# Attention scores laid out keys by queries: the maximum found beforehand, sums over keys divided out in the merge, no transposes of the exponentials

## The chip, the core and the metric

The kernel runs on one core of a Trainium2 chip. The metric is the device time in microseconds of one execution, as the median of several. The core has five engines that work side by side, each through its own list of instructions in order: TensorE (PE in the profile; its weight loads are listed apart as PEld), VectorE (DVE), ScalarE (ACT), GpSimd (POOL) and SyncE (SP), which here only starts DMA transfers. Matrix products go into PSUM, eight banks of 512 float32 columns on 128 partitions; everything else lives in SBUF.

## The reference

One encoder layer is run on two sequences with shared weights: a sample of 1024 tokens and a prompt of 256, each with 16 learned meta tokens in front. What the change touches is the attention:

```python
def attention_block(qb, k, v):
    scale = HEAD_DIM ** -0.5
    s = jnp.einsum('bqhgd,bshd->bhgqs', qb, k).astype(jnp.float32) * scale
    p = jax.nn.softmax(s, axis=-1).astype(v.dtype)
    return jnp.einsum('bhgqs,bshd->bqhgd', p, v)
...
    a = bidirectional_gqa(q, k, v) @ w_attn_o
    fo = fourier_mix(f) @ w_four_o
    merged = g_attn * a + g_four * fo
    x = x + merged @ w_out
```

There are 8 query heads of 64 features; four of them share each of 2 key heads. Queries and keys are normalised per head and rotated before. The gates `g_attn` and `g_four` are sigmoids of further columns of the input projection. A SwiGLU block with two normalisations follows; the change leaves it alone.

## The kernel before

All values are float32. A float32 factor is split into a high and a low part of the type float32r, and a product of two is three products (high by high, high by low, low by high): the helper `three`, lines 218 to 220. The program goes through stages: normalisation and Fourier input; the Fourier branch; keys, values and queries; attention; merge (gated sum of both branches) and output projection; SwiGLU. The attention stage is written out by hand: on TensorE, ScalarE and VectorE the order of the program is the order of the engine, while POOL and SP are ordered by a scheduler, as is everything after attention. SBUF is handed out as equal slots (`Slots`).

Attention works on units: a tile of 128 queries (eight of the sample, two of the prompt, which come first) and one key head. For each of the unit's four query heads, six matmuls give the scores, queries on the partitions and the 1040 keys (272 for the prompt) along the columns (line 898). High and low parts of 64 features stand on top of each other, so that each of the two products contracts over all 128 rows. VectorE finds the maximum over the keys (L903), ScalarE takes the exponential with the maximum as bias and sums it (L910), VectorE divides by the sum (L914, L915). Since the product with the values contracts over the keys, the exponentials are then turned round: for each tile of 128 keys (and one of the 16 meta keys) four transposes, one for each head (L832), a copy of the high part (L834), the low part (L835), and two products with the values (L852, L853). This second half of a unit runs between the score steps of the next one.

Between these steps the program puts matmuls of the gate logits (`gate_gen`, lines 218 to 220 under the names g, hT and wg), work that needs nothing from attention. The table `FILL` says how much after each step: 640 stands for three products of 512 columns. What is not for TensorE of that work goes to ScalarE (L443, L450) and POOL (L444). Gate products that are left over run after attention, while the first inputs of the merge are loaded (`load_af`) and split.

## Time and profile before

| what | value |
|---|---|
| median of 3 runs | 1740.58 us (1740.29 to 1740.63) |
| span of the profiled execution | 1737.8 us |
| instructions | 25952 |
| TensorE busy | 1697.8 us, 98% of the span |
| VectorE, ScalarE, POOL busy | 1140.9, 720.6, 239.6 us |
| first and last score product (L898) | 316.1 us, 637.4 us |
| first product of the merge | 670.9 us |

For the profiled execution the page gives the span, from the first to the last instruction; the median of the runs lies 2.8 us above it. In the rows of the profile, `L898 PE MATMUL S<-kT,qT` is the instruction of line 898 on TensorE that writes tile S from kT and qT; `128*128 128x264` means 128 rows contracted, 128 columns of weights, and a moving tile of 264 columns. In the timeline the first number is the start in us, the second the duration; `x6` joins six instructions that follow each other. In groups by line, the two numbers after the bar are the busy time in us and the mean duration in ns.

### The profile page before, as it was taken

How to read it: one execution, taken by the hardware profiler on the slowest of the kernel's cores; microseconds unless marked ns; L12 is line 12 of the kernel's file. 1: busy time of each engine (PE TensorE's matmuls, PEld its weight loads, DVE VectorE, ACT ScalarE, POOL GpSimd, SP SyncE). 2: the span in 40 equal slices, each digit the busy share in tenths (PEclk: the TensorE clock that was granted, in tenths of full speed). 3: DMA queues.
4: the chain of work that ended last, by engine and by line, in shares of the span. 5: the costliest groups of instructions: out<-in, count | busy, mean ns of one | idle time of the engine just before them, and what ended most of it. 6: DMA issues, size and time to landing. Idle time of an engine off the chain costs nothing.

```text
span 1737.8 us, 25952 instructions
## 1 busy us (share of the span) xinstructions
PE 1697.8 (98%) x9917; PEld 1511.1 (87%) x9917; DVE 1140.9 (66%) x2084; ACT 720.6 (41%) x1391; POOL 239.6 (14%) x239
## 2 busy tenths in 40 slices
PE   7999999999999999999999999999999999999997
...
GB/s 190 63 149 162 116 116 55 122 74 67 70 61 59 61 79 352 250 119 170 145 182 64 85 82 95 90 96 89 94 98 84 71 126 255 198 182 101 159 97 153
DMA packets 100292, 212.06 MB, mean 122 GB/s; under 512 B 10373, under 2 KB 46877, under 8 KB 100168
## 3 DMA queue, kind: packets, MB, share of 16 engines
...
## 4 chain that ended last, share of the span: by engine, by line
PE 67%; DVE 7%; DMA 3%; issue 3%; ACT 1%; POOL 1%; SPq 0%; POOLq 0%; DVEq 0%; ACTq 0%
PE i L218 9%; PE i L220 9%; PE i L219 9%; PE o L220 5%; PE o L219 5%; PE o L218 5%; PE S L898 4%; PE pt L832 4%; PE g L218 2%; PE pv L852 2%; PE g L219 2%; PE g L220 2%; PE pv L853 2%; PE wo L220 2%; PE wo L219 2%
## 5 line engine op out<-in xcount | busy, mean ns | idle before, releaser
L1227 ACT CAST w<-wi 128x512 fp32r<-128x512 f32 x168 | 104.0, 621 | 274.0 <-PE i L220 218.0
L218 PE MATMUL i<-A,w 128*128 128x384 f32 x616 | 208.4, 338 | 3.0 <-ACT w L1227 2.6
L220 PE MATMUL i<-A,w 128*128 128x384 f32 x616 | 208.1, 338 | 2.3 <-POOL w L1229 2.3
L219 PE MATMUL i<-A,w 128*128 128x384 f32 x616 | 207.9, 338 | 0.0
L218 PE MATMUL i<-Ah,w 128*128 128x256 f32 x616 | 173.0, 281 | 1.6 <-DVE sc L1283 1.5
L220 PE MATMUL i<-Ah,w 128*128 128x256 f32 x616 | 173.2, 281 | 0.0
L219 PE MATMUL i<-Al,w 128*128 128x256 f32 x616 | 172.9, 281 | 0.0
L834 ACT CAST pT<-pt 128x512 fp32r<-128x512 f32 x156 | 90.7, 582 | 97.1 <-PE pt L832 94.3
L835 DVE TENSOR_TENSOR pT<-pt,pT 128x512 fp32r<-128x512 f32 x156 | 106.9, 686 | 34.2 <-ACT pT L834 33.0
L1229 DVE TENSOR_TENSOR w<-wi,w 128x512 fp32r<-128x512 f32 x154 | 105.3, 685 | 28.7 <-ACT w L1227 28.3
L903 DVE TENSOR_REDUCE sm<-S 128x1 f32<-128x1040 f32 (+1 forms) x80 | 86.5, 1082 | 50.7 <-PE S L898 47.4
L218 PEld LDWEIGHTS i<-A,w 128*128 128x128 f32 x616 | 116.5, 189 | 3.6 <-ACT w L1227 2.9
L220 PEld LDWEIGHTS i<-A,w 128*128 128x128 f32 x616 | 116.4, 189 | 3.2 <-POOL w L1229 3.2
L218 PEld LDWEIGHTS i<-Ah,w 128*128 128x128 f32 x616 | 116.0, 188 | 2.2 <-DVE sc L1283 1.7
L219 PEld LDWEIGHTS i<-A,w 128*128 128x128 f32 x616 | 116.3, 189 | 0.0
L219 PEld LDWEIGHTS i<-Al,w 128*128 128x128 f32 x616 | 116.2, 189 | 0.0
L220 PEld LDWEIGHTS i<-Ah,w 128*128 128x128 f32 x616 | 116.0, 188 | 0.0
L227 POOL TENSOR_SCALAR fin0r<-fin0ss 128x1 f32<-128x1 f32 x1 | 0.8, 788 | 755.8 <-ACT X L235 755.8
L910 ACT ACTIVATE p<-S,sm 128x1040 f32<-128x1040 f32 (+1 forms) x80 | 80.2, 1003 | 33.6 <-DVE sm L903 27.0
L832 PE MATMUL pt<-ident,p 128*128 128x128 f32 (+1 forms) x624 | 93.4, 272 | 0.0
L220 PE MATMUL o<-wfo,act 128*128 128x512 f32 (+1 forms) x212 | 82.1, 388 | 2.1 <-DVE act L1361 2.1
L219 PE MATMUL o<-wfo,act 128*128 128x512 f32 (+1 forms) x212 | 81.9, 386 | 0.0
...
## 6 DMA issues: line engine op xcount, KB each, us to landing
...
```

The source lines that it names most:

```text
L218: mm(out, sh, mh, start=first and i == 0, stop=False)
L219: mm(out, sh, ml, start=False, stop=False)
L220: mm(out, slo, mh, start=False, stop=last and i == n - 1)
L832: nc.tensor.transpose(pt[:rows, h * P : (h + 1) * P], me.ps4[h][:, col : col + rows], self.ident[:])
L834: nc.scalar.copy(pT[:rows, :512], pt[:rows, :])
L835: nc.vector.tensor_tensor(pT[:rows, 512:1024], pt[:rows, :], f32(pT[:rows, :512]), op=ALU.subtract)
L852: nc.tensor.matmul(me.pv[:], vst, pT[:rows, :512], start=j == 0, stop=False)
L898: nc.tensor.matmul(S[:, base + lo : base + hi], hq, self.kT[seq][g][v][:, lo:hi], start=v == 0, stop=v == 1)
L903: nc.vector.tensor_reduce(nb, S[:, base : base + L], axis=AX.X, op=ALU.max, negate=True)
L910: self.last_exp = nc.scalar.activation(p, S[:, base : base + L], AF.Exp, bias=nb, accum_out=total)
L1227: nc.scalar.copy(w[:, :512], src)
L1229: eng.tensor_tensor(w[:, 512:1024], src, f32(w[:, :512]), op=ALU.subtract)
```

## The change

The scores are made the other way round: keys on the partitions, the 512 queries of the unit's four heads along the columns (L948, L949 of the new kernel). So their exponentials are already what the product with the values needs, and the transposes are gone, with the division. Three things have to be got in another way.

- **The shift.** The maximum over keys now runs across partitions. A first, coarser set of scores (high parts alone, 64 rows, queries on the partitions) is made two units ahead: matmuls in pairs, one head on rows 0 to 63 and one on rows 64 to 127 (L845, L846), four 16-column ones for the meta keys (L854), with maxima by VectorE. The negated maximum is transposed into a row (L865), and four DMAs put it below the queries' high parts as row 64; row 64 of the keys' low part is 1. So the second score product contracts 65 rows and adds the shift.
- **The sums over keys.** VectorE adds the exponentials of all key tiles into a PSUM bank (L970, L972); a product with ones sums over the partitions (L914, L915), ScalarE copies (L918), a DMA stores the row.
- **The division.** The stored sums are read back as a small tile, VectorE takes reciprocals, and they are stored again. In `load_af` products with a 0/1 table of 8 rows spread them over the heads' features (L1073, L1074), and VectorE multiplies the attention output by them (L1076), for each of the three chunks of tokens.

The low part of the exponentials moves from VectorE to POOL, the source of the cast from PSUM to SBUF. PSUM in attention becomes two banks S for the shift and the totals, two for the scores, one each for values and sums, two for gates. Queries are loaded twice in part. The fill becomes 700 after each of nine key tiles in place of 640 after each of eight half steps.

```diff
+        self.tot_d = self.dram.tile([80, P], F32, name="tot_d")
+        self.rc_d = self.dram.tile([80, P], F32, name="rc_d")
...
-    FILL = {"s": 640, "p": 400, "end": 640, "drain": 900}
+    FILL = {"s": 700, "p": 400, "end": 700, "drain": 900}
...
+            nc.gpsimd.memset(f32(k4[:rows, :, 1, 1, :]), 0.0)
+            nc.gpsimd.memset(f32(k4[:rows, :, 1, 1, 0:1]), 1.0)
             nc.scalar.copy(k4[:rows, :, 0, 0, :], kr[:rows])
-            nc.vector.tensor_tensor(k4[:rows, :, 0, 1, :], kr[:rows], f32(k4[:rows, :, 0, 0, :]), op=ALU.subtract)
-            nc.scalar.copy(k4[:rows, :, 1, 1, :], kr[:rows])
+            nc.scalar.copy(k4[:rows, :, 0, 1, :], kr[:rows])
...
+            t = tiles[i]
+            q1, q2 = sl.get("qT", F32R), sl.get("qT2", F32R)
+            nc.sync.dma_start(f32(q1[:, :1024]), self.q_d[t][:])
+            nc.sync.dma_start(f32(q2[:HD, :1024]), self.q_d[t][:HD, :])
+            odd = self.q_d[t][:HD, :].rearrange("d (g p x n) -> d g p x n", g=2, p=2, x=2)
+            for g in range(2):
+                nc.sync.dma_start(
+                    f32(q2[HD:P, g * 512 : g * 512 + 256].rearrange("d (p n) -> d p n", p=2)), odd[:, g, :, 1, :]
+                )
+            q[t] = q1, q2
...
+        def shift_work(t, g):
+            q1, q2 = q[t]
+            kt = self.kT["s" if t < 8 else "p"][g][0]
+            cuts = [(0, 512), (512, 1024)] if t < 8 else [(0, LP)]
+            parts = self.small.tile([P, 4, 4], F32, tag="parts", name=f"mx{t}{g}", bufs=3)
+            def pair(p, i):
+                lo, hi = cuts[i]
+                pp = [ps.tile([P, 512], F32, tag="S", name=f"S{t}{g}{p}{i}{x}") for x in range(2)]
+                h = 4 * g + 2 * p
+                c = g * 512 + p * P
+                nc.tensor.matmul(pp[0][:, : hi - lo], q1[:HD, h * P : (h + 1) * P], kt[:HD, lo:hi], start=True, stop=True)
+                nc.tensor.matmul(pp[1][:, : hi - lo], q2[HD:P, c : c + P], kt[HD:P, lo:hi], start=True, stop=True)
+                for x in range(2):
+                    nc.vector.tensor_reduce(parts[:, 2 * p + x, i : i + 1], pp[x][:, : hi - lo], axis=AX.X, op=ALU.max)
+            def meta():
+                pm = ps.tile([P, 512], F32, tag="S", name=f"S{t}{g}m")
                 for h in range(4):
+                    c = (4 * g + h) * P
+                    nc.tensor.matmul(
+                        pm[:, h * N_META : (h + 1) * N_META], q1[:HD, c : c + P], kt[:HD, SEQ_S:LS], start=True, stop=True
+                    )
+                nc.vector.tensor_reduce(
+                    parts[:, :, 2], pm[:, : 4 * N_META].rearrange("p (h n) -> p h n", h=4), axis=AX.X, op=ALU.max
+                )
+            nb = self.small.tile([P, 4], F32, tag="nb", name=f"nb{t}{g}", bufs=3)
+            def row():
+                pt = ps.tile([P, 512], F32, tag="S", name=f"S{t}{g}r")
+                nc.tensor.transpose(pt[:4, :P], nb[:], self.ident[:])
+                mr = self.small.tile([4, P], F32R, tag="mr", name=f"mr{t}{g}", bufs=1)
+                nc.vector.tensor_copy(mr[:], pt[:4, :P])
+                for h in range(4):
+                    c = (4 * g + h) * P
+                    nc.sync.dma_start(f32(q2[HD : HD + 1, c : c + P]), f32(mr[h : h + 1, :]))
+            for i in range(len(cuts)):
+                for p in range(2):
+                    pair(p, i)
+                    yield
+            if t < 8:
+                meta()
+            n = 3 if t < 8 else 1
+            nc.vector.tensor_reduce(nb[:], parts[:, :, :n], axis=AX.X, op=ALU.max, negate=True)
+            yield
+            row()
+            yield
...
+        def total(unit):
+            t, g, st = unit
+            b = ps.tile([P, 512], F32, tag="S", name=f"S{t}{g}t")
+            a = st["a"]
+            nc.tensor.matmul(b[:2, :], self.ones[:], a[:, :512], start=True, stop=False)
+            nc.tensor.matmul(b[:2, :], self.ones[:], a[:, 512:1024], start=False, stop=True)
+            sl.put(a)
+            s = sl.get("tot")
+            nc.scalar.copy(s[:1, :512], b[:1, :])
+            r = t * NQH + 4 * g
+            nc.sync.dma_start(self.tot_d[r : r + 4, :].rearrange("(o h) n -> o (h n)", o=1), s[:1, :512])
+            sl.put(s)
...
-                nc.vector.tensor_reduce(nb, S[:, base : base + L], axis=AX.X, op=ALU.max, negate=True)
...
-                self.last_exp = nc.scalar.activation(p, S[:, base : base + L], AF.Exp, bias=nb, accum_out=total)
...
-                    nc.vector.reciprocal(rc, total)
-                    nc.vector.tensor_scalar(p, p, rc, None, op0=ALU.mult)
...
+            if i + 2 < len(units):
+                load_q(tiles.index(units[i + 2][0]))
+                shifts.append([shift_work(*units[i + 2]), 7 if units[i + 2][0] < 8 else 5])
+            st = {}
+            unit = t, g, st
+            q1, q2 = q[t]
+            n = len(kk)
+            if g == 0 and t in (5, 6):
+                (self.load_totals if t == 5 else self.invert_totals)((0, 2))
+            two = None
+            for j, (V, rows, col) in enumerate(kk):
+                pst = ps.tile([P, 512], F32, tag="st", name=f"st{t}{g}{j}")
+                c = slice(g * 512, (g + 1) * 512)
+                kt = self.kT[seq][g]
+                nc.tensor.matmul(pst[:rows, :], kt[0][:, col : col + rows], q1[:, c], start=True, stop=False)
+                nc.tensor.matmul(
+                    pst[:rows, :], kt[1][: HD + 1, col : col + rows], q2[: HD + 1, c], start=False, stop=True
+                )
+                if 0 < j < 3 and todo:
+                    todo.popleft()()
+                if two is None:
+                    two, x = sl.get("P"), 0
+                pj = two[:rows, x * 512 : (x + 1) * 512]
+                pT = sl.get("pT", F32R)
+                self.last_exp = nc.scalar.activation(pj, pst[:rows, :], AF.Exp)
+                nc.scalar.copy(pT[:rows, :512], pj)
+                nc.gpsimd.tensor_tensor(pT[:rows, 512:1024], pj, f32(pT[:rows, :512]), op=ALU.subtract)
+                if add:
+                    add()
+                def add(unit=unit, j=j, rows=rows, pj=pj, free=two if x or j == n - 1 else None):
+                    t, g, st = unit
+                    if j == 0:
+                        st["acc"] = ps.tile([P, 512], F32, tag="acc", name=f"acc{t}{g}")
+                        nc.vector.tensor_copy(st["acc"][:], pj)
+                    else:
+                        nc.vector.tensor_tensor(st["acc"][:rows, :], st["acc"][:rows, :], pj, op=ALU.add)
+                    if free:
+                        sl.put(free)
+                if x or j == n - 1:
+                    two = None
+                x = 1
+                late.append((unit, j, pT))
+                if shifts:
+                    left = n - j
+                    gen, k = shifts[0]
+                    for _ in range(-(-k // left)):
+                        next(gen, None)
+                        shifts[0][1] -= 1
+                    if j == n - 1:
+                        run_all(gen)
+                        shifts.popleft()
+                if len(late) > 3:
+                    second(*late.popleft())
+                yield "end" if i + 1 == len(units) else seq, 0, True
...
+            def sums(st=st):
+                a = st["a"] = sl.get("acc2", F32R)
+                nc.scalar.copy(a[:, :512], st["acc"][:])
+                nc.vector.tensor_tensor(a[:, 512:1024], st["acc"][:], f32(a[:, :512]), op=ALU.subtract)
+            todo.append(sums)
+            todo.append(lambda unit=unit: total(unit))
...
+    def invert_totals(self, chunks):
+        for c in chunks:
+            n = 8 * len(CH_TILES[c])
+            r = self.totals.pop(c)
+            self.nc.vector.reciprocal(r[:n, P : 2 * P], r[:n, :P])
+            self.nc.sync.dma_start(self.rc_d[32 * c : 32 * c + n, :], r[:n, P : 2 * P])
+            self.sl.put(r)
+    def head_scales(self, c):
+        nc, sl = self.nc, self.sl
+        n = CH_N[c]
+        raw, hl, sel = sl.get("rc"), sl.get("rch", F32R), sl.get("sel", F32R)
+        rows = self.rc_d[32 * c : 32 * c + n // 16, :].rearrange("(t h) n -> h t n", h=NQH)
+        nc.sync.dma_start(raw[:NQH, :n].rearrange("h (t n) -> h t n", n=P), rows)
+        nc.gpsimd.dma_start(sel[:NQH, :512], self.a["sel"])
+        nc.scalar.copy(hl[:NQH, :n], raw[:NQH, :n])
+        nc.vector.tensor_tensor(hl[:NQH, n : 2 * n], raw[:NQH, :n], f32(hl[:NQH, :n]), op=ALU.subtract)
+        sl.put(raw)
+        return hl, sel
...
+                for j in range(per):
+                    k = i * per + j
+                    pb = self.mm[0].tile([P, 512], F32, tag=self.mm[1], name=f"rc{c}{k}")
+                    w = sel[:NQH, k * P : (k + 1) * P]
+                    nc.tensor.matmul(pb[:, :n], w, hl[:NQH, :n], start=True, stop=False)
+                    nc.tensor.matmul(pb[:, :n], w, hl[:NQH, n : 2 * n], start=False, stop=True)
+                    rk = raws[0][:, j * n : (j + 1) * n]
+                    nc.vector.tensor_tensor(rk, rk, pb[:, :n], op=ALU.mult)
...
-        with self.psum("pd", {"S": (1, 1536), "tr": 2, "pv": 1, "g": 2}) as ps:
+        with self.psum("pd", {"S": 2, "st": 2, "pv": 1, "acc": 1, "g": 2}) as ps:
...
+            self.load_totals((1,))
+            self.invert_totals((1,))```

The next rows are TensorE's list in attention, in a sample unit. Before: the scores of a head, a key tile's transposes and value products, and the next transposes (pt is a transposed tile of exponentials, pv the product with the values).

```order
L898 MATMUL S_4430<-kT_2491,pT_3960 128x264
L898 MATMUL S_4430<-kT_2492,pT_3960 128x264
L898 MATMUL S_4430<-kT_2491,pT_3960 128x512
L898 MATMUL S_4430<-kT_2492,pT_3960 128x512
L898 MATMUL S_4430<-kT_2491,pT_3960 128x264
L898 MATMUL S_4430<-kT_2492,pT_3960 128x264
L832 MATMUL pt_4439<-ident,p_4222 128x128 x2
L832 MATMUL pt_4439<-ident,p_4315 128x128
L832 MATMUL pt_4439<-ident,p_4222 128x128
L852 MATMUL pv_4284<-pT_4398,v_2498 128x512
L853 MATMUL pv_4284<-pT_4398,v_2498 128x512
```

After: one key tile of a unit, the third, at which the totals of the unit before come too (st is the tile of scores, S11t the totals, S_4643 and S_4644 a pair of the shift).

```order
L948 MATMUL st_4628<-qT_4159,kT_2493 128x512
L949 MATMUL st_4628<-qT_624_4160,kT_2494 128x512
L914 MATMUL S11t<-acc_713_4605,ones 2x512
L915 MATMUL S11t<-acc_713_4605,ones 2x512
L845 MATMUL S_4643<-kT_2493,qT_4567 128x512
L846 MATMUL S_4644<-kT_2493,qT_708_4568 128x512
L893 MATMUL pv_4470<-pT_4557,v_2501 128x512
L894 MATMUL pv_4470<-pT_4557,v_2501 128x512
L220 MATMUL g_2_4595<-hT2h_490,wgh_4214 128x256
```

The pair stands alone between products over 65 and 128 rows; it comes in the first four tiles of a unit, the meta products in the fifth, the transposed shift in the sixth.

The second place is TensorE's list in the merge, where the last products of one unit of chunk 0 (tile m) are followed by those of the next. Before:

```order
L218 MATMUL m_7207<-afh_6883,mh_1107_7113 128x512
L219 MATMUL m_7207<-afl_6899,mh_1107_7113 128x512
L220 MATMUL m_7207<-afh_6883,ml_1074_6940 128x512
L218 MATMUL m_7294<-wmh_6845,ml_1074_6940 128x512
L219 MATMUL m_7294<-afl_6861,ml_1074_6940 128x512
```

After, the reciprocals' products of chunks 1 and 2 (tile rc) stand between them:

```order
L222 MATMUL m_7426<-afh_7102,ml_1264_7159 128x512
L1073 MATMUL rc_7476<-rch_7465,sel_7466 128x512
L1074 MATMUL rc_7476<-rch_7465,sel_7466 128x512
L1073 MATMUL rc_7480<-rch_7465,sel_7466 128x512
L1074 MATMUL rc_7480<-rch_7465,sel_7466 128x512
L1073 MATMUL rc_7489<-rch_7465,sel_7466 128x512
L1074 MATMUL rc_7489<-rch_7465,sel_7466 128x512
L1073 MATMUL rc_7493<-rch_7465,sel_7466 128x512
L1074 MATMUL rc_7493<-rch_7465,sel_7466 128x512
L1073 MATMUL rc_7525<-rch_7516,sel_7517 128x256
```

and on VectorE, in the same place of the new program, the operations that empty the banks:

```order
L1150 TENSOR_TENSOR gt_7329<-m_7426,gt_7329 128x512
L1076 TENSOR_TENSOR af_7460<-af_7460,rc_7476 128x512
L1151 TENSOR_TENSOR gt_7329<-gt_7329 128x512
L1076 TENSOR_TENSOR af_7460<-af_7460,rc_7480 128x512
L1076 TENSOR_TENSOR af_7471<-af_7471,rc_7489 128x512
L1154 TENSOR_TENSOR ml_1311_7412<-gt_7329,wmh_7048 128x512
L1076 TENSOR_TENSOR af_7471<-af_7471,rc_7493 128x512
L1037 TENSOR_TENSOR rch_7516<-rc_7515,rch_7516 8x256
L205 TENSOR_TENSOR ml_1264_7159<-af_7460,mh_1297_7332 128x1024
L1076 TENSOR_TENSOR af_7511<-af_7511,rc_7525 128x256
```

The products of chunk 2 wait for the split rch_7516, which VectorE reaches only after it has used those of chunk 1.

136 lines of the change are left out of this document (46 added, 90 removed).

## The prediction

> **What bounds the kernel now.** First the head of the profile page, for the share of each engine.
>
> ```profile
> span 1737.8 us, 25952 instructions
> PE 1697.8 (98%) x9917; PEld 1511.1 (87%) x9917; DVE 1140.9 (66%) x2084; ACT 720.6 (41%) x1391; POOL 239.6 (14%) x239
> ```
>
> TensorE is busy 98% of the span. Then the busy times of five stretches: attention on the prompt tiles, on the sample tiles, its drain with the last gate products, and two pieces of the merge.
>
> ```profile
> core 0: us, PE busy (x) PEld busy (x) DVE busy (x) ACT busy (x) POOL busy (x), PEclk, DMA share, GB/s
> 316.00:356.00 40.00, 38.63 (x229) 32.46 (x230) 20.75 (x57) 20.82 (x57) 7.74 (x6) 1.00 0.36 114
> 356.00:640.00 284.00, 281.10 (x1715) 240.07 (x1714) 219.43 (x327) 177.51 (x322) 28.33 (x22) 1.00 0.21 63
> 640.00:671.00 31.00, 30.89 (x180) 25.16 (x179) 17.21 (x24) 18.96 (x31) 7.09 (x4) 1.00 0.76 245
> 700.00:720.00 20.00, 19.39 (x84) 15.44 (x83) 19.96 (x18) 9.02 (x12) 7.13 (x3) 1.00 0.57 198
> 720.00:760.00 40.00, 36.59 (x206) 31.12 (x205) 31.93 (x49) 19.74 (x27) 12.62 (x5) 1.00 0.64 216
> ```
>
> In the sample part TensorE is busy for 281.1 of 284 us at the full clock, while VectorE has 65 us free and ScalarE 107. The gate products fill TensorE there, and they must be done in any case. So a score product saved is a microsecond saved, and one added is one lost. VectorE is the full engine only at 700 to 720, in the merge. Of TensorE's waits by line, one falls in attention:
>
> ```profile
> PE S L898 <- ACT p L910: 4.1, 6, 1.2
> ```
>
> **What TensorE pays before.** A matmul's own duration contains its pipeline's tail, so I price by distances between starts. TensorE's timeline: a head's scores, a plain key tile, the 16 meta keys, and gate products of 256 columns.
>
> ```profile
> 600.76 1.12 PE L898 MATMUL S<-kT,qT 128*128 128x264 f32 x6
> 601.71 0.60 PE L832 MATMUL pt<-ident,p 128*128 128x128 f32 x4
> ...
> 645.55 0.60 PE L832 MATMUL pt<-ident,p 128*128 128x128 f32 x4
> 646.08 0.49 PE L852 MATMUL pv<-pT,v 16*128 16x512 f32 x1
> 646.41 0.39 PE L853 MATMUL pv<-pT,v 16*128 16x512 f32 x1
> 646.74 0.50 PE L218 MATMUL g<-hT1h,wgh 128*128 128x512 f32 x1
> 647.07 0.40 PE L219 MATMUL g<-hT1h,wgh 128*128 128x512 f32 x1
> ...
> 651.41 0.60 PE L832 MATMUL pt<-ident,p 128*128 128x128 f32 x4
> 651.77 0.48 PE L852 MATMUL pv<-pT,v 128*128 128x512 f32 x1
> 652.08 0.39 PE L853 MATMUL pv<-pT,v 128*128 128x512 f32 x1
> 652.31 0.39 PE L218 MATMUL g<-hT1h,wgh 128*128 128x512 f32 x1
> 652.54 0.39 PE L219 MATMUL g<-hT1l,wgh 128*128 128x512 f32 x1
> ...
> 657.84 0.28 PE L218 MATMUL g<-hT2h,wgh 128*128 128x256 f32 x1
> 657.95 0.28 PE L219 MATMUL g<-hT2l,wgh 128*128 128x256 f32 x1
> ```
>
> - Six score products of a head, 2080 columns: 601.71 - 600.76 = 0.95 us.
> - A 512-column product: 652.54 - 652.31 = 0.23; a 256-column one 0.11 to 0.12.
> - A key tile (four transposes, two value products): 652.31 - 651.41 = 0.90, so the transposes are 0.90 - 2 x 0.23 = 0.44.
> - The same work where the products contract over only 16 rows: from the transposes to the second gate product 647.07 - 645.55 = 1.52, against 652.54 - 651.41 = 1.13. **Entering and leaving a product that uses fewer rows of the array costs 0.39 us** for the visit, here before the first such product, before the next, and after the last. This row decides the case.
>
> A sample unit (one query tile, one key head) is 4 x 0.95 + 8 x 0.90 + 0.90 + 0.39 = 12.29 us. With 24 gate products of 0.23 (5.5) it is 17.8, times 16 units 285: the window above has 284, so the prices hold. A prompt unit: eight score products of 272 columns at 0.126 (between 0.12 and 0.23, by columns), two key tiles, the meta tile: 1.0 + 1.80 + 1.29 = 4.1.
>
> **What TensorE pays after, per sample unit.**
> - Scores, keys by queries: 9 key tiles x 2 x 0.23 = 4.14. The 16 meta keys cost as much as 128, since the moving side is the 512 queries. The second product contracts 65 rows; I take it as a full-array product.
> - Value products: 9 x 2 x 0.23 + 0.39 = 4.53, as before but without 36 transposes.
> - Shift: four pairs of 64-row products of 512 columns and a visit of four 64-row products of 16 columns. Each pair stands between full-array products (the order shown above), so each is a visit. No row has 64 rows; the nearest are the 16-row ones, so I take 0.39 a visit. Whether the two of a pair, on different halves of the array, overlap is not in the trace either: 0.23 if wholly, 0.46 if not; I take 0.34, half, since the visit row shows that a product after a change waits even for its own kind (646.41 - 646.08 = 0.33). Four pairs: 4 x 0.73 = 2.92, bounds 2.48 to 3.40. The meta visit: 0.39 and four short products, taken as transposes (0.11): 0.83, bounds 0.49 to 0.83, I take 0.69.
> - The transposed shift 0.15, the two products that sum over keys 0.46.
>
> Sum 12.89, bounds 12.3 to 13.5, against 12.29. **The 36 transposes (4.0 us) are gone, but their place is taken by the shift.** Times 16: +9.6 us, bounds -1 to +20.
>
> Prompt units: 6 x 0.23 + 6 x 0.23 + 0.39, two pairs with one to two visits (0.85), 0.15 and 0.46: 4.6 against 4.1, times 4 is +2. The reciprocals' products in the merge: eight of 512 columns for each large chunk (16 x 0.23 = 3.7) and eight of 256 (0.9) make 4.6; they contract 8 rows and stand alone in chunk 0 (four visits) and together in the others (one): 5 x 0.39 = 2.0. So +6.6. **TensorE's work: +18 us, bounds +5 to +31.**
>
> The Trainium skill, TensorEngine Tiling (Array Packing), Key Properties, says that changing the tiling mode, not merely the tile, drains the engine; by that the 64-row visits would be priced like the 16-row one, and the trace's 0.39 agrees for 16 rows. The skill's TensorE: Matmul & The Clock Gate, Part 3, has matmuls in different row groups start about 4 ns apart; by that a pair costs 0.23, the sum falls by 16 x 4 x 0.11 = 7 us, to about 1768; no run here shows it.
>
> **What else moves.** The next rows are groups by line and form.
>
> ```profile
> L903 DVE TENSOR_REDUCE sm<-S 128x1 f32<-128x1040 f32 x64 | 79.5, 1242 | 37.1 <-PE S L898 37.1
> L903 DVE TENSOR_REDUCE sm<-S 128x1 f32<-128x272 f32 x16 | 7.0, 440 | 13.5 <-PE S L898 10.3 <-PE pt L832 1.8 <-ACT wgh L443 1.4
> L910 ACT ACTIVATE p<-S,sm 128x1040 f32<-128x1040 f32 x64 | 72.4, 1132 | 20.1 <-DVE sm L903 17.1 <-DVE sm L914 3.0
> L910 ACT ACTIVATE p<-S,sm 128x272 f32<-128x272 f32 x16 | 7.8, 488 | 13.6 <-DVE sm L903 9.9 <-DVE sm L914 3.5
> L835 DVE TENSOR_TENSOR pT<-pt,pT 128x512 fp32r<-128x512 f32 x136 | 93.4, 687 | 27.7 <-ACT pT L834 26.5
> L834 ACT CAST pT<-pt 16x512 fp32r<-16x512 f32 x20 | 11.3, 564 | 3.7 <-PE pt L832 3.7
> L443 ACT CAST wgh<-wg 128x512 fp32r<-128x512 f32 x60 | 36.1, 622 | 27.2 <-DMA wg<-w_g 17.4 <-PE f L219 4.8 <-DVE qs L775 1.5
> L444 POOL TENSOR_TENSOR wgl<-wg,wgh 128x512 fp32r<-128x512 f32 x28 | 36.1, 1291 | 253.6 <-ACT wgh L443 203.4 <-PE pt L832 49.5 <-issue 0.5
> L1037 DVE TENSOR_TENSOR gt<-m,gt 128x512 f32<-128x512 f32 x16 | 10.9, 681 | 0.0
> L203 DVE TENSOR_TENSOR afl<-af,afh 128x1024 fp32r<-128x1024 f32 x6 | 7.3, 1219 | 2.7 <-ACT afh L202 2.7
> ```
>
> Per sample unit TensorE now needs 12.9 plus gates. The fill of 700 at nine steps against 640 at eight gives 5.5 x 6300 / 5120 = 6.8: 19.7 us. Against that:
> - ScalarE: an exponential of 512 columns lies on the line between 488 and 1132 at 0.69; nine of these and nine casts from SBUF (0.62) are 11.8, three more copies 1.7, gate work about 2: 15.5.
> - VectorE: a 512-column maximum by the same line 0.69, eight are 5.5; nine additions into the sums at 0.69, 6.2; with the rest 12.8.
> - POOL: nine low parts at 1.29 are 11.6, with the gates' 13.7; before it had about 1.8.
>
> None reaches 19.7, so edits on these three cost nothing while TensorE's 19.7 covers them; without that cover the excess over the next, ScalarE, would be what is left.
>
> Waits that the change adds on TensorE:
> - The sums' product takes one of the two S banks, and the pair right behind it needs both. It waits for ScalarE to copy the total (0.56 by the 16x512 row, with hand-over about 0.8, of which the pair's first product covers some): 0.5 in 14 units, 7 us, bounds 0 to 14.
> - In the prompt units the sample's pairs come three in a row; each waits for the two maxima of the one before (2 x 0.69) less its own time: about 2.3 us in two units and 0.4 in two others, 5.5, bounds 0 to 9. The 4.1 us of the row of waits go.
> - The query tile for the pair is loaded at the start of the unit that needs it, and the shift travels by DMAs on SP behind stores of sums and outputs; the last sums go out and come back by DMA before their reciprocal, with chunk 0's scaling behind that on VectorE. Gate products cover these: I take 3, bounds 0 to 8.
> - In the merge the twelve products stand in a row on TensorE, the last four behind a split that VectorE reaches late. On VectorE: seven operations of 0.68, one of 0.41, two of 1.2 and one of 0.4 stand until the bank of the next merge product is free, some 8 us against TensorE's own 3; VectorE was full there (19.96 of 20). I take 5, bounds 2 to 8.
>
> Together 7 + 5.5 - 4.1 + 3 + 5 = **+16 us**, bounds -2 to +35. Sum +18 + 16 = +34. The profiled execution's span is 1737.8, so its after is 1772; the median lies 2.8 above the span (start and end, untouched): 1740.6 + 34 = **1775 us**.
>
> **Rivals.**
> 1. *The shift is nearly free, and the kernel gets faster.* If a 64-row visit costs nothing and pairs overlap, a sample unit falls to 4.14 + 4.53 + 4 x 0.23 + 0.1 + 0.15 + 0.46 = 10.3, 32 us less over 16 units. With +6.6 and +16 beside it that is 1731, with the waits at their low end 1716. With pairs half overlapped it turns only when visits cost almost nothing: 91 visits (80 in sample units, 6 in prompt, 5 in the merge) at 0.39 are 35 us, as much as the loss; with full overlap the turn is at 0.08 a visit. Against it stands the 0.39, for it that no row has 64 rows. Chance 0.13.
> 2. *The 65-row score product counts as a change of mode too.* Then 9 x 16 + 3 x 4 = 156 more visits of 0.39: +61, 1836. The trace has only 128 and 16 rows to go by; 65 is the nearer to 16. Against it: more than half of the array is in use, so nothing could stand beside it. Chance 0.07. The skill's TensorEngine Tiling (Array Packing), Tiling Modes, lists tiles of 32, 64 and 128 rows; no run here shows what 65 rows take.
> 3. *A feeder becomes the bound*: the shift's row or the query load comes late in every sample unit. Two microseconds each would be 32 more, less the 3 counted: 1804. For it: POOL's work grows sevenfold and SP gets about 140 more DMAs (four rows of shift and one of sums in each of 20 units, and more query loads); against it: the shift is asked for two units ahead. Chance 0.10.
>
> If the added waits hide and pairs overlap wholly, 1775 - 18 - 7 = 1750: that is still the forecast, at its lower end.
>
> **How the numbers follow.** Forecast 0.70, rival 1 0.13, rival 2 0.07, rival 3 0.10. Sums of the bounds give 1740.6 + 5 - 2 = 1744 to 1740.6 + 31 + 35 = 1807; rival 3 lies within. I give 1742 to 1812, leaving out rivals 1 and 2, two in ten. A measurement of this kernel can tell about 0.2% (3.5 us). Faster 0.14, within 0.2% 0.04 (the low ends of forecast and the high end of rival 1), slower 0.82.
>
> **What would show it.** On TensorE's timeline of the sample units: the start-to-start distance from a score product through a pair to the next value product, 0.23 + 0.73 by me; 0.46 and no more by rival 1. The plain pair of score products at 0.46, not 0.85 (rival 2). The sample part must be longer than 284 us by about 30 (19.7 x 16 = 315), though with more gate products in it, and the drain after it shorter by up to 20. Waits of TensorE: on ScalarE's copy of the totals some 7 us; on VectorE's maxima in the prompt units; in the merge on VectorE's products by the reciprocals. If TensorE shows gaps of microseconds on a DMA in each unit, rival 3 holds. The forecast fails if pairs cost 0.3 or less all told.

## The result, and the profile after

The changed kernel takes **1840.36 us** (1836.62 to 1846.88 in four runs) against 1740.43 for the one before on the same chip: a ratio of 1.058, 95% interval 1.0559 to 1.0601. I had predicted slower, but 1775 us and no more than 1812.

The head of the page, the mean granted clock, and the busy times in the same stretches as shown of before, then attention's longer rest, its drain, and the merge:

```profile
span 1838.0 us, 25903 instructions
PE 1754.3 (95%) x9481; PEld 1492.3 (81%) x9481; DVE 1119.2 (61%) x2071; ACT 759.8 (41%) x1430; POOL 441.1 (24%) x421
```

```profile
core 0: 1838.0 us, clock 0.972
```

```profile
core 0: us, PE busy (x) PEld busy (x) DVE busy (x) ACT busy (x) POOL busy (x), PEclk, DMA share, GB/s
316.00:356.00 40.00, 30.29 (x115) 18.36 (x116) 19.54 (x44) 13.11 (x23) 12.11 (x10) 0.84 0.27 77
356.00:640.00 284.00, 254.26 (x1037) 171.72 (x1035) 147.92 (x250) 160.18 (x280) 151.94 (x120) 0.90 0.22 64
640.00:733.00 93.00, 90.40 (x416) 64.97 (x416) 51.76 (x84) 67.18 (x119) 65.94 (x53) 1.00 0.27 78
733.00:760.00 27.00, 22.02 (x102) 16.31 (x101) 17.59 (x20) 15.02 (x20) 9.87 (x7) 0.87 0.86 286
760.00:886.00 126.00, 120.38 (x594) 99.59 (x594) 96.84 (x138) 52.05 (x68) 40.49 (x17) 0.96 0.56 189
```

By the first and last products on TensorE's timeline the loss has one place. From the first score product to the first product of the merge it was 316.1 to 670.9 us, 354.8; it is 314.2 to 760.1, 445.9: **+91**. The merge, to the first product of the output projection, went from 116.6 to 126.0: +9. All the rest together is the same.

Before, TensorE was busy for 281.1 of 284 us in the sample part, at full clock. Now it is busy for 254.3, and the column PEclk stands at 0.90: both the work is interrupted and the work runs slower. The mean clock was 0.997 and is 0.972. A stretch at half clock loses half its length, so the span times what is missing to 1 bounds the loss: 1838.0 x 0.028 = 51 us against 1737.8 x 0.003 = 5. In the windows above, attention alone has 40 x 0.16 + 284 x 0.10 + 27 x 0.13 = 38. **Up to 46 of the 100 us are clock**, and no step of the prediction had the clock in it.

TensorE's waits by line (total, number and longest of them): the first two fall in attention and are on one load.

```profile
PE S L846 <- DMA qT<-q_d: 19.4, 8, 5.6
PE S L845 <- DMA qT<-q_d: 13.4, 6, 5.6
...
PE S L846 <- ACT tot L918: 3.5, 14, 0.3
PE g L220 <- DVE af L1076: 3.2, 1, 3.2
...
PE rc L1073 <- DVE gt L1149: 2.7, 1, 2.7
...
PE S L845 <- DVE mx L848: 2.0, 4, 0.8
```

32.8 us of waits for the query tile, where I had taken 3 for this load, the shift's row and the last sums together. One of them on the timeline, with SP's transfers, TensorE's products, POOL's low parts of the exponentials and, in brackets, how long an engine was idle and what ended it:

```profile
417.59 0.28 DVE L867 CAST mr<-S11r 4x128 fp32r<-4x128 f32 x1 [0.51 <-PE S11r L865]
417.90 3.16 SPq L870 DMA_DIRECT2D qT<-mr  x4
...
421.04 2.54 POOL L961 TENSOR_TENSOR pT<-P,pT 128x512 fp32r<-128x512 f32 x2 [0.93 <-ACT pT L960]
...
421.33 0.35 SPq L818 DMA_DIRECT2D qT<-q_d  x1
...
423.60 0.49 SPq L819 DMA_DIRECT2D qT<-q_d  x1
423.70 0.40 PE L949 MATMUL st<-qT,kT 65*128 65x512 f32 x1
424.14 1.28 SPq L822 DMA_DIRECT2D qT<-q_d  x2
424.81 0.46 PE L845 MATMUL S<-kT,qT 64*128 64x512 f32 x1 [0.71 <-DMA qT<-q_d]
427.38 0.47 PE L846 MATMUL S<-kT,qT 64*128 64x512 f32 x1 [2.11 <-DMA qT<-q_d]
...
428.41 0.63 PE L220 MATMUL g<-hT1h,wgh 128*128 128x512 f32 x1
428.84 0.63 PE L221 MATMUL g<-hT1h,wgh 128*128 128x512 f32 x1
```

SP works its list in order. The four DMAs of the shift's row (L870) can start only when VectorE has cast the row, near the end of a unit; the next tile's four loads (L818 to L822) stand behind them. But the row has gone out by 417.90 + 3.16 = 421.06, and the loads then wait for memory: their slots are still in use. L818 starts as a value product (L894) ends at 421.30, and L819 as POOL's low parts do (421.04 + 2.54 = 423.58); the two small loads (L822) stand behind L819. SP's own waits name both:

```profile
SPq L819 <- POOL pT L961: 6.8, 5, 2.1
...
SPq L818 <- PE pv L894: 2.6, 4, 1.5
```

The last load is issued after 424.14. The pair of the new tile is TensorE's next work at 423.9, and waits twice. In the five tiles whose load waits for POOL so, TensorE's waits come to 18.6 of the 32.8 us. Then the clock goes: two gate products start 428.84 - 428.41 = 0.43 us apart where 0.23 is normal, and a finer window shows it:

```profile
424.00:428.00 4.00, 1.18 (x4) 0.59 (x4) 0.80 (x2) 2.07 (x4) 2.39 (x2) 1.00 0.49 136
428.00:432.00 4.00, 4.00 (x12) 2.74 (x11) 1.87 (x3) 0.03 (x1) 0.00 (x0) 0.57 0.00 0
```

### The profile page after: what moved, and what is told of

It is laid out like the page before. It is cut to its first block, busy times and chain, and to the rows that moved or that the text cites. A ratio compares the mean times of both kernels' runs of the same rounds, so it can differ in the third digit from the quotient of the medians.

```text
span 1838.0 us, 25903 instructions
## 1 busy us (share of the span) xinstructions
PE 1754.3 (95%) x9481; PEld 1492.3 (81%) x9481; DVE 1119.2 (61%) x2071; ACT 759.8 (41%) x1430; POOL 441.1 (24%) x421
## 4 chain that ended last, share of the span: by engine, by line
PE 80%; DVE 6%; DMA 5%; ACT 3%; issue 3%; POOL 3%; SPq 1%; POOLq 0%; ACTq 0%; DVEq 0%
PE i L220 9%; PE i L222 9%; PE i L221 9%; PE o L222 4%; PE o L221 4%; PE o L220 4%; PE g L220 4%; PE g L222 4%; PE g L221 3%; PE pv L893 2%; PE pv L894 2%; PE st L948 2%; PE st L949 2%; DMA qT<-q_d 2%; PE m L220 1%
## 5 line engine op out<-in xcount | busy, mean ns | idle before, releaser
L961 POOL TENSOR_TENSOR pT<-P,pT 128x512 fp32r<-128x512 f32 x156 | 199.4, 1282 | 187.0 <-ACT pT L960 157.8
L220 PE MATMUL i<-A,w 128*128 128x384 f32 x616 | 208.5, 339 | 3.2 <-ACT w L1340 2.9
L222 PE MATMUL i<-A,w 128*128 128x384 f32 x616 | 208.1, 338 | 1.8 <-POOL w L1342 1.8
L221 PE MATMUL i<-A,w 128*128 128x384 f32 x616 | 208.2, 338 | 0.0
L220 PE MATMUL i<-Ah,w 128*128 128x256 f32 x616 | 174.4, 283 | 2.3 <-DVE sc L1396 2.3
L222 PE MATMUL i<-Ah,w 128*128 128x256 f32 x616 | 174.4, 283 | 0.0
L221 PE MATMUL i<-Al,w 128*128 128x256 f32 x616 | 173.7, 282 | 0.0
L848 DVE TENSOR_REDUCE mx<-S 128x1 f32<-128x512 f32 (+1 forms) x144 | 90.8, 659 | 91.0 <-PE S L846 50.8
L959 ACT ACTIVATE P<-st 128x512 f32<-128x512 f32 x156 | 92.7, 594 | 119.3 <-PE st L949 99.7
L972 DVE TENSOR_TENSOR acc<-acc,P 128x512 f32<-128x512 f32 (+1 forms) x136 | 94.3, 693 | 66.6 <-ACT P L959 66.3
L220 PEld LDWEIGHTS i<-A,w 128*128 128x128 f32 x616 | 116.7, 190 | 3.8 <-ACT w L1340 3.2
L220 PEld LDWEIGHTS i<-Ah,w 128*128 128x128 f32 x616 | 116.9, 190 | 2.5 <-DVE sc L1396 2.5
L222 PEld LDWEIGHTS i<-A,w 128*128 128x128 f32 x616 | 116.3, 189 | 2.8 <-POOL w L1342 2.7
L221 PEld LDWEIGHTS i<-Al,w 128*128 128x128 f32 x616 | 117.2, 190 | 0.0
L222 PEld LDWEIGHTS i<-Ah,w 128*128 128x128 f32 x616 | 116.8, 190 | 0.0
L221 PEld LDWEIGHTS i<-A,w 128*128 128x128 f32 x616 | 116.4, 189 | 0.0
L960 ACT CAST pT<-P 128x512 fp32r<-128x512 f32 x156 | 96.8, 620 | 7.9 <-DMA a_d<-ao 0.6
L222 PE MATMUL o<-wfo,act 128*128 128x512 f32 (+1 forms) x212 | 82.1, 388 | 1.5 <-DVE act L1474 1.5
L220 PE MATMUL o<-wfo,act 128*128 128x512 f32 (+1 forms) x212 | 81.5, 388 | 0.4 <-ACT act L1473 0.4
```

The lines of the kernel that those rows point to most:

```text
L220: mm(out, sh, mh, start=first and i == 0, stop=False)
L221: mm(out, sh, ml, start=False, stop=False)
L222: mm(out, slo, mh, start=False, stop=last and i == n - 1)
L848: nc.vector.tensor_reduce(parts[:, 2 * p + x, i : i + 1], pp[x][:, : hi - lo], axis=AX.X, op=ALU.max)
L959: self.last_exp = nc.scalar.activation(pj, pst[:rows, :], AF.Exp)
L960: nc.scalar.copy(pT[:rows, :512], pj)
```

## The experiments

Stage times are worked out as above; the clock is the profiled execution's mean. Each ratio is against runs of the kernel before on the same chip.

| kernel | us | ratio to before, 95% | attention | merge | clock |
|---|---|---|---|---|---|
| before | 1740.4 | | 354.8 | 116.6 | 0.997 |
| after | 1840.4 | 1.0559-1.0601 | 445.9 | 126.0 | 0.972 |
| early | 1802.4 | 1.0336-1.0382 | 406.2 | 127.0 | 0.984 |
| full | 1804.9 | 1.0354-1.0385 | 410.7 | 126.3 | 0.980 |
| early_full | 1783.4 | 1.0236-1.0266 | 390.5 | 126.2 | 0.987 |
| early_full_unit | 1851.8 | 1.0624-1.0659 | 464.4 | 121.6 | 0.966 |
| before_late | 1741.8 | 1.0002-1.0021 | 355.7 | 117.4 | 0.997 |
| noshift | 1751.2 | 1.0050-1.0082 | 357.7 | 124.1 | 0.985 |
| spread | 1790.5 | 1.0273-1.0305 | 394.2 | 126.9 | 0.986 |
| norc | 1777.2 | 1.0203-1.0234 | 383.0 | 125.5 | 0.987 |
| notot | 1751.4 | 1.0047-1.0081 | 364.0 | 121.4 | 0.989 |
| nodiv | 1729.9 | 0.9920-0.9956 | 343.5 | 120.0 | 0.993 |
| noshift_nodiv | 1710.6 | 0.9815-0.9855 | 324.2 | 118.0 | 0.989 |
| column | 1782.9 | 1.0228-1.0262 | 385.2 | 127.3 | 0.990 |
| column_thin | 1804.2 | 1.0354-1.0385 | 409.3 | 128.1 | 0.984 |
| column_slot | 1737.1 | 0.9976-0.9995 | 342.2 | 130.2 | 0.991 |
| column_slot_pv2 | 1741.5 | 1.0000-1.0019 | 342.5 | 132.0 | 0.992 |
| best_a | 1737.3 | 0.9973-0.9990 | 340.7 | 130.9 | 0.994 |
| best_b | 1741.2 | 1.0000-1.0018 | 340.7 | 130.9 | 0.993 |
| best_d | 1738.6 | 0.9984-1.0003 | 347.4 | 124.8 | 0.993 |

### The load, and the pairs on two row halves

Theory A in the expectations is that the late load, with the clock that its waits halve, is what the prediction missed. Three kernels test it: the load one tile earlier; the shift's scores over all 128 rows (high and low part of the queries times the high part of the keys), one head after the other, which drops the two small loads; and both.

```diff
 # early
-                load_q(tiles.index(t) + 1)
+                load_q(tiles.index(t) + 2)
 # full
-                nc.tensor.matmul(pp[0][:, : hi - lo], q1[:HD, h * P : (h + 1) * P], kt[:HD, lo:hi], start=True, stop=True)
-                nc.tensor.matmul(pp[1][:, : hi - lo], q2[HD:P, c : c + P], kt[HD:P, lo:hi], start=True, stop=True)
+                for x in range(2):
+                    c = (h + x) * P
+                    nc.tensor.matmul(pp[x][:, : hi - lo], q1[:, c : c + P], kt[:, lo:hi], start=True, stop=True)
```

> The query tile is loaded one tile (two units) earlier; nothing else changes. Theory A (the loss is the late query load, 32.8 us of TensorE waits on that DMA, and the halved clock that follows such waits, some 75 us at half speed inside attention, 38 us lost): both go, 1840 - 33 - 38 = 1769 us (1757 to 1781), TensorE waits on the load under 3 us, clock above 0.99. Theory B (TensorE's added work and the row of the shift are the loss; behind the load stands another wait): above 1800 us, the waits reappear at the shift's row or at POOL.

> The shift's scores contract all 128 rows (queries' high and low parts against keys' high parts), one head after the other; so no product with 64 rows is left, and two of the four query loads fall away. The load stays late. Theory A: the 64-row visits are worth about 18 us by the distances of the changed kernel (64 pairs at 0.62 against 0.46, 16 meta visits 0.4 dearer), the two small loads some of the waits: 1800 to 1822 us, clock still below 0.985. Theory B: TensorE's added work is most of the loss, so 1790 us or less.

> Both edits. Theory A: they add, 1769 - 18 = 1751 us (1740 to 1763). If the pairs on two halves of the array were worth having, this is slower than the early load alone, above 1769.

The early load gains **38 us**: real, but about half of what I then expected, and 1802 lies in theory B's range. One wait on the load is left in `early`, of 4.2 us, but the clock is 0.984 and not above 0.99: other waits bring stretches at half clock too. `full`, its load still late, gains 35, as expected; with two of the four loads gone TensorE's waits on the load are 14.5 us and not 32.8. In the four sample tiles from 418 to 540 us they are 5.1, against 13.0 in the same tiles of the changed kernel, though the shift's row still stands ahead; so the small loads behind the slot are the larger part there. The two gains overlap: together they are 57, and `early_full` is 20 us slower than its upper bound. With the load early, full rows gain another 19 (1802 to 1783). A pair in the changed kernel, where it waits for nothing:

```profile
663.43 0.40 PE L948 MATMUL st<-qT,kT 128*128 128x512 f32 x1
663.66 0.40 PE L949 MATMUL st<-qT,kT 65*128 65x512 f32 x1
663.99 0.50 PE L845 MATMUL S<-kT,qT 64*128 64x512 f32 x1
664.00 0.50 PE L846 MATMUL S<-kT,qT 64*128 64x512 f32 x1
664.43 0.50 PE L893 MATMUL pv<-pT,v 128*128 128x512 f32 x1
664.76 0.39 PE L894 MATMUL pv<-pT,v 128*128 128x512 f32 x1
665.00 0.39 PE L220 MATMUL g<-hT1h,pT 128*128 128x512 f32 x1
```

The two of a pair start together, so they overlap wholly. From L949 to the gate product it is 1.34 us; without a pair it would be three products, 0.69. So a pair costs **0.65** where I took 0.73 and two full-row products cost 0.46. The row also answers rival 2: the 65-row product starts 0.23 after the 128-row one.

What is left of the 43 us over the kernel before is, by `early_full`'s waits, no longer a load:

```profile
PE S L841 <- ACT tot L913: 4.4, 14, 0.4
PE S00m L849 <- DVE mx L843: 4.1, 1, 4.1
...
PE S91t L909 <- DVE mx L843: 3.0, 1, 3.0
```

### Was it the load's place, or what stood ahead of it?

The kernel before, with its load moved to the start of the tile:

```diff
 # before_late
-        load_q(0)
...
-                load_q(tiles.index(t) + 1)
+                load_q(tiles.index(t))
```

> The kernel before with one edit: a tile's queries are loaded when the tile begins, as in the changed kernel, where the kernel before loads them a tile ahead. Theory A (the wait for a load that stands behind other work on SP is what costs, and each wait of some 3.4 us brings a stretch at half clock): ten tiles, each waiting 2 to 4 us for its load, 20 to 40 us in all, and several stretches at half clock in the records on top: 1765 to 1800 us. Theory B (the halved clock belongs to the changed kernel's own products, not to the waits): waits of the same size but no new stretch at half clock: 1760 at most. If the old order of work hides the load, 1740 to 1745, and then neither is told apart.

1741.8: no change that counts, and the third case of the expectation, by which the theories are not told apart. TensorE's waits name the load, for a microsecond:

```profile
PE S L896 <- DMA qT<-q_d: 1.0, 2, 0.5
```

So the same place in the program does little harm to this load. It is a single DMA into a single slot, with no row on SP ahead of it; in the changed kernel it is four DMAs into two slots. So the place alone does not make it late. How much the row and how much the slots make of it was not separated: the trace above and `full` put the larger part, in the middle tiles, on the slots. That waits also halve the clock of the old kernel was not shown by this run.

### The division

First another way to divide, in the unit: the ones are 128 columns wide, VectorE takes the reciprocals of the 128x512 sums out of the S bank, and the value product is multiplied when it is emptied.

```diff
 # early_full_unit
-            nc.scalar.copy(s[:1, :512], b[:1, :])
+            nc.vector.reciprocal(s[:, :512], b[:])
...
-            nc.scalar.copy(aos[:, :512], pv[:])
+            nc.vector.tensor_tensor(aos[:, :512], pv[:], st["rc"][:, :512], op=ALU.mult)
```

> Both edits, and the sums over keys are divided out inside attention: the product with ones has 128 columns, so that the sums stand on all partitions, VectorE takes reciprocals of 128x512 and multiplies when it empties the value product; no sums go through memory, no products of 8 rows in the merge. Theory A (the merge pays 9 us for the reciprocals, its wait on VectorE and clock, and their products 6): 1735 us (1725 to 1745), below the kernel before. Rival: the reciprocal of 512 columns holds VectorE and the S bank, and a wait of 1 us a unit takes its place: 1751 us or more.

The rival came true. A reciprocal of that size takes five times what an addition does, and holds the bank that the next pair needs:

```profile
L914 DVE RECIPROCAL tot<-S80t x1: 3356/3356/3356, 333.8 to 333.8; 128x512 f32<-128x512 f32 x1
```

```profile
PE S L841 <- DVE tot L914: 48.8, 17, 3.3
```

Then the division left out piece by piece from `early_full`. `norc` drops what uses the sums (reciprocals, the products that spread them, the multiplications); `notot` also the totals' product, its copy and store; `nodiv` also the split of the sums into two parts.

```diff
 # nodiv (norc: only the last two; notot: total() reduced to giving its slot back)
-            todo.append(sums)
-            todo.append(lambda unit=unit: total(unit))
...
-            self.load_totals((1,))
-            self.invert_totals((1,))
...
-                    nc.tensor.matmul(pb[:, :n], w, hl[:NQH, :n], start=True, stop=False)
```

> early_full (query tile loaded a tile earlier, shift's scores over all 128 rows) without the division: no split of the sums, no totals' product, no sums through memory, no reciprocals, no products that spread them, the output stays unscaled (the output is another function then). The additions of the exponentials stay. By early_full's profile the totals' product with its wait is 16 units of about 0.75 us, 12 to 16 us with the wait of 0.3, and the merge's share 9.5: 1783 - 22 = 1761. If the totals also hold up the shift's banks (S00m, S91t and others wait there for VectorE), up to 10 more: 1750.

> early_full with the sums, their split and the totals' products kept in attention, but without what uses them: no reciprocals, no products that spread them, the output stays unscaled (another function). It splits the 53 us that leaving the whole division out won. By early_full's profile the merge's side is 126.1 - 119.9 = 6 us in the merge, about 4.6 of products ahead of it and 5 of waits around them: 15, so 1768, and attention's side is the other 38. Rival: the merge's side is most of it: 1740 to 1750.

> norc (1777) without the totals' products and their copies as well, but with the split of the sums on ScalarE and VectorE, whose result nothing reads then (the output stays unscaled, another function). Leaving out all of the division gave 1730, so 47 us lie between the two. If the totals' products and the S bank that they take are the cause: 1730 to 1740. If the split's 16 x (0.6 + 0.7) us on ScalarE and VectorE, in front of exponentials and maxima, is the cause: 1760 to 1777.

1783.4, 1777.2, 1751.4, 1729.9: in this order the use of the sums costs 6, the totals' products 26, the split 22, **53.5 in all**, and without them the changed form beats the kernel before by 10. `nodiv` is 20 us faster than the furthest that I expected, `norc` gained less than either reading had it, and both expectations for `notot` failed; each had one cause for all of it. That the split costs so much was not in my sums at all: ScalarE and VectorE had time to spare on the mean of a unit. But it comes in the unit's first key tiles, ahead of the maxima on VectorE's list, and `notot`'s waits show who pays:

```profile
PE S L841 <- DVE mx L843: 7.7, 12, 3.0
```

In `nodiv` this row is 2.3. The longest of these waits on VectorE's timeline:

```profile
367.19 0.69 DVE L983 TENSOR_TENSOR acc<-acc,acc 128x512 fp32r<-128x512 f32 x1 [4.83 <-ACT acc L982]
...
368.52 1.28 DVE L843 TENSOR_REDUCE mx<-S 128x1 f32<-128x512 f32 x2
```

VectorE stands idle until ScalarE has copied the high part (L982), and the maxima of a pair whose products began at 362.73 stand behind that and the split. Not all of the 4.83 us is the split's doing: ScalarE came late there itself, with an exponential that started at 364.90. The clock takes more: 1749.7 x 0.011 - 1730.4 x 0.007 = 7 us at most. That names some 12 of the 22; the rest I have not placed.

### The shift

The search for the shift left out of the changed kernel, its load kept at the late place; and the same without the division.

```diff
 # noshift
-            for g in range(2):
-                nc.sync.dma_start(
...
+            nc.gpsimd.memset(f32(q2[HD : HD + 1, :1024]), 0.0)
...
-                shifts.append([shift_work(*units[i + 2]), 7 if units[i + 2][0] < 8 else 5])
...
-                self.last_exp = nc.scalar.activation(pj, pst[:rows, :], AF.Exp)
+                self.last_exp = nc.scalar.activation(pj, pst[:rows, :], AF.Exp, scale=0.1)
```

> The changed kernel without the search for the shift: no pairs, meta products, maxima, row transposes, row DMAs or small query loads; the shift row is set to zero and the exponentials are taken of a tenth of the scores so that they stay finite (the output is another function then). The query load keeps its late place. The prediction put the search at 16 visits and their products, 2.9 us of TensorE in a sample unit (16 units, 46 us) and some 10 in the prompts. If the search only costs its own TensorE time, 1840 - 56 = 1784 with the load waits unchanged. Theory A: with the four row DMAs gone from SP the load is no longer late either (most of 33 us of waits and 38 us of half clock go with them): 1715 to 1740. Rival 1 of the prediction (the shift for nothing) gave 1716 to 1731.

> The changed kernel without the shift (as noshift, exponentials of a tenth of the scores) and without the division: what the reorganised scores, exponentials and value products take alone. From noshift's 1751: if the division costs on its own what it cost beside the shift (53), 1698; if it costs so much only where the shift stands beside it on the S banks and on VectorE, 1751 - 25 = 1726 (9 of totals' products, 5 of the merge's products, 11 of waits around them).

The search costs 89 us in the changed kernel, the load's wait included; 1751 lies between the two readings. The late load makes TensorE wait once, for 2.2 us. That says nothing on why it was late: without pairs the new tile is not wanted until two units after its load. Without division too, the reorganised form takes 1711, again between the two readings and 29 less than before; the division costs 41 here, against 53.5 beside the shift, so most of it does not come from meeting the shift. With the shift search gone the units are short, and TensorE waits for ScalarE instead (`PE pv L889 <- ACT ao L895`, 20.9 us in `noshift`). From `noshift_nodiv` to `nodiv` the search costs 19 with the load early and rows full. That is no clean price: `noshift_nodiv` has the lower clock of the two (0.989 against 0.993), so it pays for waits of its own.

### More filling in the prompts' stage

```diff
 # spread
-    FILL = {"s": 700, "p": 400, "end": 700, "drain": 900}
+    FILL = {"s": 610, "p": 1500, "end": 610, "drain": 900}
```

> early_full with the gates' filling set to 1500 a step in the prompt units (400 before) and 610 a step in the sample units (700): the same gate products, more of them between the steps where the shift of the first two sample units is crowded into twelve prompt steps. Theory: the prompts' stage loses some 15 us to VectorE's maxima, which more filling covers, and with it two stretches at half clock: 1783 - 15 = 1768. Rival: the waits only move to the sample units, whose filling is now thinner: 1778 to 1790.

1790.5: the rival, at its upper end. Moving gate products only moved the waits: from 314 to 375 us TensorE is busy for 54.10 of 61 us, where `early_full` has 46.58, and from 375 to 640 for 251.15 of 265, where it has 256.72, at a clock of 0.94 in place of 0.99.

### Sums from the value product

If the division costs what it does on ScalarE, VectorE and in the S bank, taking the sums from a product that is made anyway should give that back. One of the value tile's 128 columns (the low part of feature 63) becomes 2^-30, so that the sums come out as a row of the value product.

```diff
 # column
+            nc.gpsimd.memset(f32(V[:rows, :, 1, e:HD]), TINY)
...
-                if add:
-                    add()
+                if x or j == n - 1:
+                    sl.put(two)
 # column_slot, in place of the last two lines
+                if held:
+                    sl.put(held)
+                held = two if x or j == n - 1 else None
```

> early_full with the sums made another way: one column of the values' low part (feature 63 of each key head) is replaced by 2^-30, so that row 127 of the value product is the sum of the exponentials times 2^-30, stored with the product; the reciprocals are multiplied by 2^-30. Gone are the additions on VectorE, the split of the sums, the totals' products and their copies; the bank of the additions becomes a third bank for the shift's scores. The low part of that one feature is lost, and the rest computes the reference. The division's reciprocals and their products in the merge stay. Theory (the division's place in attention, totals' products and VectorE's additions, is most of the 53 us that leaving the division out won): near that kernel's 1730, plus the merge's share of about 10, less a few for the third bank and VectorE's 6 us in each unit: 1730 to 1745. Rival (the merge's share is most of the 53): 1760 to 1780.

> As column, with 640 of gate filling a step in the sample units in place of 700, as in the kernel before: fewer gate products between the steps, more of them left for the drain behind attention, where the last sums and the reciprocals are waited for. If the tail's wait is what costs, 2 to 6 us less than column; if the units are short of filling, 2 to 10 more.

> As column, but the slot of two exponential tiles is given back one key tile later, as the additions did it. In column's profile the exponentials wait 54.9 us for POOL's low parts (the groups by line), and TensorE 31 us for the exponentials and for the copy of the value product behind them: a slot given back at once is taken again for the next tile while POOL still reads it. If that is what ate column's gain, the waits go and the theory's number comes back: 1730 to 1745. If ScalarE and POOL were short anyway: 1770 to 1783.

> As column_slot, with the bank that the additions leave given to the value product (two) and not to the shift's scores (two, not three). If what is left of TensorE's waits is on the copy of the value product, it is 2 to 6 us less than column_slot; if on VectorE's maxima in the prompt units, 2 to 8 us more.

`column` gained nothing: 1782.9 is past the rival's range too, and the merge's share is not the cause, but a new wait that I had put in. The exponentials of `column`, grouped by line and form (the releasers of idle time stand last):

```profile
L957 ACT ACTIVATE P<-st 128x512 f32<-128x512 f32 x136 | 81.0, 596 | 67.4 <-POOL pT L959 40.0 <-PE st L947 12.1 <-DMA a_d<-ao 6.4
```

and of `column_slot`:

```profile
L957 ACT ACTIVATE P<-st 128x512 f32<-128x512 f32 x136 | 81.2, 597 | 71.5 <-PE st L947 51.9 <-PE S L844 6.3 <-DMA a_d<-ao 4.2
```

A slot given back at once is taken again while POOL still reads it. Given back one key tile later, ScalarE waits for TensorE in the main, and TensorE has next to nothing to wait for:

```profile
375.00:640.00 265.00, 264.61 (x1292) 210.80 (x1290) 77.23 (x144) 191.34 (x333) 201.22 (x159) 1.00 0.27 82
```

264.61 of 265 us at full clock, and **46 us less** than `column` for a slot held one key tile longer. 1737.1 is as fast as the kernel before (a ratio of 0.9985, inside the 0.2% that I count as no change). Less filling (`column_thin`) cost 21 more, twice what its expectation had at most; a second bank for the value product did 4 worse than a third for the shift.

### What is left, in the merge

`column_slot`'s attention is 13 us shorter than before's, and its merge 14 longer. `best_a` puts the scaling of chunks 1 and 2 between the last products of chunk 0's merge and the additions of the halves on POOL; `best_b` begins one step earlier, behind every second group; `best_d` scales chunk 2 among the last gate products.

```diff
 # best_a
-                run_all(self.load_af(c))
+                yield from self.load_af(c)
...
+                        if i >= 7 and k % 1 == 0 and 0 in chunks and steps < 9:
+                            next(then)
+                            steps += 1
...
-                nc.vector.tensor_tensor(r, r, x, op=ALU.add)
+                nc.gpsimd.tensor_tensor(r, r, x, op=ALU.add)
 # best_d
-            for _ in af:
+            for _ in chain(af, self.load_af(2)):
                 gates(1300)
```

> column_slot (1737) with the merge's division spread out: in the last step of chunk 0's merge one piece of the scaling of chunks 1 and 2 stands behind each group of products, where it stood in one row ahead of them, and the additions of the two halves go from VectorE to POOL. column_slot's merge takes 130 us against 117 before, with 13.7 us of half clock behind waits of TensorE on VectorE's multiplications. If that row of products is the cause: 4 to 8 us less, 1729 to 1733. If VectorE as a whole is short in the merge, only its two additions of 1.2 us are won: 1734 to 1737.

> As best_a, but the pieces begin one step earlier and stand behind every second group of products. By the first theory another 1 to 3 us less than best_a; if POOL's additions or the earlier use of memory slots hold up the weights, 2 to 5 more.

> best_a (1737) with chunk 2's scaling (the prompts', whose sums are known long before) taken out of the merge and put behind chunk 0's, among the last gate products. In best_a's merge, between 680 and 720 us of the span, TensorE is busy for 33.8 of 40 us and a stretch of 13.7 us runs at half clock; this takes four of the twelve reciprocals' products and a third of VectorE's work away from there. If the crowding there is what costs: 3 to 6 us less, 1731 to 1734. If it only moves into the drain, where gate products run out: 1736 to 1740.

None gains. `best_b` is 4 us slower than `best_a`, as its second case had it. `best_d` does shorten the merge by 6, to 124.8, and attention's end takes it back: there TensorE waits 4.2 us for the load of the 0/1 table. In `best_a` two stretches of the merge:

```profile
680.00:700.00 20.00, 16.02 (x66) 11.86 (x64) 18.84 (x14) 7.65 (x10) 17.42 (x7) 0.99 0.52 179
700.00:720.00 20.00, 17.78 (x53) 11.67 (x52) 16.80 (x24) 8.55 (x11) 1.35 (x1) 0.67 0.74 246
```

VectorE is busy for 18.84 of 20, TensorE falls to 16, and the clock halves behind it. But POOL is busy for 17.42 there, and the wait just before the half clock is on POOL. Two of its rows, and the two largest rows of TensorE's waits from 640 to 800 us:

```profile
689.63 5.67 POOL L1050 TENSOR_TENSOR af<-af,af 128x1024 f32<-128x1024 f32 x2
695.26 2.80 POOL L206 TENSOR_TENSOR wmh<-wm,ml 128x1024 fp32r<-128x1024 f32 x1
```

```profile
PE m L223 <- POOL wmh L206: 2.5, 1, 2.5
PE m L223 <- POOL ml L206: 2.4, 2, 1.5
```

The two additions that I had moved to POOL (L1050) stand ahead of a split (L206) that the next merge products need. TensorE's waits on VectorE fall from some 10 us in `column_slot` to 4.5, and those on POOL rise from 1 to 4.9. So the time lies at the upper end of the second reading, but its cause, VectorE short as a whole, is not shown: waits were traded. In the kernel before, VectorE was full there already (19.96 of 20 at 700 to 720). Whether the changed form can be made the faster one in the merge stays open.

## Why the prediction was wrong

**The step that failed: "Gate products cover these: I take 3, bounds 0 to 8".** The load cost 32.8 us of waits, and moving it forward gained 38 us. Gate products behind a waiting pair cover nothing, since TensorE takes its list in order; they cover only if they stand ahead of it, and the pair stood near the start of the new tile's first unit. I had counted some 140 more DMAs on SP, and named the stores that the shift's row travels behind, but not that the loads stand behind the row, whose own start waits for VectorE, and not that their slots are still being read when they are wanted, by TensorE and POOL. `early` shows what the lateness costs; what each of the two adds to it stays open.

**The term that was missing: the clock.** In the changed kernel's trace, seven of the nine tiles' load waits come with a stretch at half clock; at most 46 of the 100 us are clock, and `early` and `early_full` show that not all of it is the load's. Every window that I read of the profile before stood at full clock (its mean is 0.997). It did hold the price, outside attention: a wait of 2.63 us behind eight transposes, and a granted clock (PEclk) of 0.53 in the 7 us after it.

```profile
909.82 0.44 PE L218 MATMUL i<-A,w 128*128 128x384 f32 x1 [2.63 <-ACT w L1227]
910.00:917.00 7.00, 4.90 (x16) 4.39 (x17) 6.28 (x5) 2.64 (x6) 6.92 (x6) 0.53 0.22 74
```

**The division, 28 us in my sums, measured 53.5.** Totals' products and S bank: 9.2 + 7 = 16, measured 26. Their use in the merge: 6.6 + 5 = 12, measured 6. The split: nothing, measured 22. "None reaches 19.7, so edits on these three cost nothing" compares means over a unit; `notot` shows the maxima late behind one more operation in the wrong place, and `column` shows the same of POOL.

**The prompts' three pairs, 5.5, bounds 0 to 9: too small.** TensorE was busy for 38.63 of 40 us there before; with the load early, `early_full` still has, from 314 to 375 us,

```profile
314.00:375.00 61.00, 46.58 (x184) 29.20 (x183) 34.98 (x72) 26.84 (x50) 22.77 (x18) 0.90 0.32 93
```

14 us idle and 0.10 of the clock. In `nodiv` TensorE is busy for 55.7 of these 61, and in `notot` for 50.64, so the division makes most of it, the split more than the totals' products.

**What held.** A pair that waits for nothing takes 0.65, inside my bounds (0.62 to 0.85), and the sum's 0.73 was 5 us too much in 64 pairs. The 65-row product changes nothing. The visits were priced rightly: full rows in their place, with two loads fewer in each tile, gain 19 once the load is early. The rest of the new products is not what the change loses by: `nodiv` has full-row scores and the same value products, and is faster than before. The merge, 5 us of waits and some 3 of products, measured 9.

**The rivals.** Rival 3 was the right one, at a chance of 0.10: the query load came late in nearly every sample tile, with 14 waits of 2.3 us on the mean where I had put 2 for each of 16. Its 1804 lacks the clock; adding attention's 38 us gives 1842. That this meets 1840 is partly chance, since the division was underpriced too and some of the clock belongs to it. Rival 2 had the time, 1836, for a reason that the trace refutes. Rival 1 was right that pairs overlap, and wrong that a visit is free: a pair takes 0.65 where it needed 0.23. (Its low end is 1713 by its own terms, not 1716.) A time below its range, 1711, comes only with the shift and the division left out.

The Trainium skill, TensorE: Matmul & The Clock Gate, Part 3, The mechanism, by which the prediction worked out a pair at 0.23 us beside its sum, has matmuls on different row groups start some 4 ns apart. The trace agrees, at 0.01 us in the rows above (663.99 and 664.00). The visit around them is paid even so.
